# In-projection statistics from rows of x squared in their own layout, and the first loads and splits in another order

## The chip, the cores and the metric

The kernel runs on one core of a Trainium2 chip. A core has five engines with their own instruction streams: TensorE (PE in the profile, its weight loads PEld), VectorE (DVE), ScalarE (ACT), GpSimd (POOL) and SyncE (SP), which here only issues transfers (DMAs). They meet through semaphores. Operands lie in SBUF (128 partitions); products come out in PSUM, eight banks of 128x512 fp32.

The metric is the device time of one execution in microseconds (us). Three runs of the kernel before took 2518.49, 2518.77 and 2519.21 us: a median of 2518.77.

## The reference

One layer of an encoder over 2048 tokens of width 1024, with a memory of 256 tokens:

```python
xn = rmsnorm(h, g_mix[l])
z = jnp.einsum('bsd,dc->bsc', xn, w_in[l])          # q, k, v, p_in, f_logit
...                                                  # forgetting attention and multi-scale pool
h = h + jnp.einsum('bsc,cd->bsd', jnp.concatenate([fox, pool], axis=-1), w_out[l])
mn = rmsnorm(mem, g_mem_kv[l])
mkv = jnp.einsum('bmd,dc->bmc', mn, w_mem_kv[l])     # keys and values of the memory
...                                                  # cross-attention on the memory
...                                                  # SwiGLU
```

where `rmsnorm(x, g)` is x / sqrt(mean(x^2) + 1e-6) * g over the 1024 channels of a token. So each of the 2048 tokens of x, and each of the 256 of the memory, needs one number, the inverse root of the mean of its squares. The change is about how these numbers come about.

## The kernel before

All large products are computed in three passes: each operand is split into a high part (rounded to the fp32r format) and a low part (the rest), and `mm3` (lines 66 to 71) issues high by high, high by low and low by high. L69, L70 and L71 in the profile are these three passes, whatever the product. ACT makes the high part, DVE the low part (`split`, `split_gain`, L185 and L186, `sub_hi`, L64). The gains of the norms are multiplied into the weights while they are split; the token's own factor is multiplied on when a product leaves PSUM (`scaled`, L354), so a product may run before its statistics are known.

The stage in question has two parts. In the first, PE computes the memory's keys and values: tiles `kv00`, `kv01`, `kv10`, `kv11` (first digit: half of the 256 memory tokens; second: keys or values), each in its own bank, over eight steps k of 128 channels. Per step there are 12 matmuls of 128x512. The weights `w_mem_kv` come in eight loads of 512 KB (`load_kv`), and `split_kv` puts their parts in turn into `qs`, `kh` and `kl`. The memory comes transposed in four tiles of 256 KB (`x_load` with `memT`), each holding two steps. 22 warm-up matmuls on zeros stand ahead of it on PE.

The second part is the in-projection of x: 16 blocks of 128 tokens, each of 96 matmuls (four column groups `zps` of 384 or 392, eight steps k, three passes). x comes transposed, 256 tokens at a time, as four tiles (`x_load`), and `x_split` makes `xhi` and `xl` of them. So block i belongs to the pair b = i // 2. Its weights are eight loads of 772 KB (`load_w_in`), split by `split_w_in` into `wh` and `wl`. Block 0 (`zps0`) runs with k outermost, so that each step needs only the weights of that k; later blocks run column group by column group. The four `zps` tiles take over the four banks of the `kv` tiles: the first that of bank 4, the second bank 7, the third bank 6, the fourth bank 5; `kv00` to `kv11` lie in 4, 5, 6, 7 in the order in which line 225 makes them.

The statistics lie across the partitions of the transposed x, so they need a sum over partitions. `x_split` squares each tile on ACT (L167), POOL adds the four up into `part` (L169) and folds its two halves (L171), and `token_sums` multiplies `part` by a column of ones on PE (L211). `token_rstd` copies the two sums out of PSUM on DVE (L217) and takes the inverse root on POOL (L78, L80). For the memory the same stands at k=3, with its sums over `mpart`.

Between lines 223 and 576 all five engines follow the order in which the code is written (`in_order`); within that stretch each engine's stream is this order, and an instruction that waits holds all behind it on its engine. SP issues its loads and stores in this order too. After the stretch a scheduler sets the order on all engines but PE, whose order stays as written within the listed engines.

In the loop over blocks, per block: loads for later; the first column group of block i; the last transposes of block i-2; on even blocks `token_sums`; the other column groups; ACT's `scaled`; transposes of block i-1 (`to_heads`, L406); then `normed_heads`, and for even blocks `x_split` of the next pair, for odd ones a split of the pool weights `w_p`.

Of the kernel before, what the change touches and what calls it, by code (L numbers as in the profile page):

```python
# [16 lines left out]
P = 128  # L17
# [24 lines left out]
def block_kernel(ctx: ExitStack, tc: tile.TileContext, x, xT, memT, cols, rows, w_qkvf, w_p, w_pool, w_out,  # L42
# [116 lines left out]
    def x_split(tiles, part=None, qs=range(4), join=True):  # L159

        for q in qs:
# [3 lines left out]
            if part is not None:  # L165
                sq = xp.tile([P, 2, B], F32, tag="xsq", name="xsq", bufs=2)[:] if q else part
                act.activation(sq, raw[:], AF.Square, scale=1.0 / 32.0)  # L167
                if q:
                    pool.tensor_tensor(out=part, in0=part, in1=sq, op=ALU.add)  # L169
                if q == 3 and join:  # L170
                    pool.tensor_tensor(out=part[:, 0], in0=part[:, 0], in1=part[:, 1], op=ALU.add)  # L171
# [29 lines left out]
    with ExitStack() as c0:  # L201
# [4 lines left out]
        def token_sums(part, halves=1):  # L206

            ssp = tpp.tile([P, 2], F32, tag="ss", name="ss", bufs=1)
            for j in range(2):
                for c in range(halves):  # L210
                    pe.matmul(ssp[:, j:j + 1], lhsT=part[:, c, j * P:(j + 1) * P], rhs=ones[:, 0:1], start=c == 0,  # L211
                              stop=c == halves - 1)
            return ssp

        def token_rstd(ssp, outp):
            ms = xp.tile([P, 2], F32, tag="ms", name="ms", bufs=2)
            dve.tensor_copy(ms[:], ssp[:])  # L217
            rsqrt(outp, ms[:])


# [4 lines left out]
        kv = [[kvp.tile([P, MW], F32, name=f"kv{m}{a}") for a in range(2)] for m in range(2)]  # L225
# [8 lines left out]
        def load_kv(k):  # L234
            wk[k] = w_in_hi(k, F32)[:, :2 * MW]
            sp.dma_start(wk[k], w_mem_kv[k * P:(k + 1) * P, :])

        def split_kv(k):
# [3 lines left out]
            w_ = MW if k == 0 else 2 * MW  # L242
# [24 lines left out]
        for k in range(4):  # L267
            mt += x_load(0, memT.rearrange("(k p) m -> p k m", p=P), (k,))
            load_kv(k)
        xt = x_load(0)  # L270
        mpart = xp.tile([P, 2, B], F32, tag="part", name="part", bufs=1)
        mr = cst.tile([P, 2], F32, name="mr")
        for k in range(KD):
            if k == 0:
                raw = mt[0][1]
                x_split(mt, None, (0,))
# [13 lines left out]
            if k < 4:  # L290
                load_kv(k + 4)
            if k == 1:
                sp.dma_start(rowt[:], rows.partition_broadcast(P))
                load_w_in(0)
            if k == 3:
                for c in range(1, KD):
                    load_w_in(c)
# [42 lines left out]
        with ExitStack() as c1:  # L340
# [84 lines left out]
            def load_w_p(k):  # L425
# [3 lines left out]
                else:  # L429
                    raw = xp.tile([P, 2, B], F32, tag="xsq" if k == NPRE else "part", name="wpr",  # L430
                                  bufs=2 if k == NPRE else 1)
# [6 lines left out]
            def stat_diag(b):  # L438

                diag = xp.tile([P, 2, B], F32, tag="xsq", name="diag", bufs=2)[:, 0].rearrange("p (j t) -> p j t", j=2)  # L440
# [10 lines left out]
            def stat_rows(rbp):  # L451
                rb = xp.tile([P, 2, B], F32, tag="xsq", name="rbs", bufs=2)[:, 0]
# [49 lines left out]
            NPRE = 6  # L502
# [1136 lines left out]
```

## Time and profile before

| | |
|---|---|
| Median of three runs | 2518.77 us |
| Profiled execution | 2518.27 us |
| Its span, first to last instruction | 2516.6 us |
| Mean granted TensorE clock | 0.999 |
| PE busy | 2496.4 us |
| DVE, ACT, POOL busy | 1674.5, 1235.0, 800.5 us |
| First `kv` matmul starts | 6.56 us |
| First `zps` matmul starts | 34.46 us |
| Block 1's first matmul starts | 52.23 us |

Rows of the timeline give the start, the duration, the engine, the line and operation, the tile written, the tiles read, the shape and a count; in brackets stands how long the engine had been idle and what ended that. Where a count is over one, the duration spans all of them. Rows of groups give the total busy time in us and the mean of one instruction in ns, then the idle time ahead of them. Consecutive matmuls overlap: the step from one start to the next is their cost, not the duration.

### The profile page before, as it was taken

To read this page: it belongs to the slowest core of one execution; us is meant where nothing else is said; L and a number is where in the kernel's file an instruction comes from. 1 tells how busy PE (TensorE), PEld (TensorE's weight loads), DVE (VectorE), ACT (ScalarE), POOL (GpSimd) and SP (SyncE) were. 2 spreads that over 40 slices of the span, in tenths; PEclk is the share of its full clock that TensorE was granted. 3 is DMA by queue.
4 is the path that set the end of the run, shared out by engine and by line. 5 is a ranking of instruction groups with operands and counts; after the bars stand their busy time and mean duration, and the time that the engine had idled before them with its cause. 6 is when DMAs were issued, how large, how long until landed. Compare 5 with 4: busy or idle time off the path is not lost.

```text
span 2516.6 us, 36820 instructions
## 1 busy us (share of the span) xinstructions
PE 2496.4 (99%) x13055; PEld 2139.7 (85%) x13055; DVE 1674.5 (67%) x2971; ACT 1235.0 (49%) x2355; POOL 800.5 (32%) x1096
## 2 busy tenths in 40 slices
PE   9999999999999999999999999999999999999999
PEld 8999999878888878888888888888888888888887
DVE  7444485579999965545877787657776666665554
ACT  6454451069999945444634433335443333333443
POOL 3344310035655623334244454330001222212000
PEclk9999999999999999999999999999999999999999
DMA  6454475366665432223644554457673323325765
GB/s 249 155 155 130 122 239 168 130 189 159 149 184 155 111 115 80 75 88 126 236 178 168 184 181 167 163 206 265 225 256 106 109 99 125 112 97 183 239 205 205
DMA packets 209688, 408.25 MB, mean 162 GB/s; under 512 B 24928, under 2 KB 100448, under 8 KB 198624
## 3 DMA queue, kind: packets, MB, share of 16 engines
q1 hardware_dynamic: 179392, 309.41, 38.8%
q0 software_dynamic: 30112, 96.49, 10.6%
q8 instruction: 102, 1.67, 0.3%
q14 instruction: 82, 0.67, 0.1%
HBM read 277.24 MB, written 132.78 MB: 163 GB/s over the span
## 4 chain that ended last, share of the span: by engine, by line
PE 72%; issue 9%; DVE 2%; POOL 1%; ACT 1%; DMA 1%; POOLq 0%; SPq 0%; ACTq 0%; DVEq 0%
PE bk L71 14%; PE bk L69 14%; PE bk L70 14%; PE acc L865 5%; PE sps L791 5%; PE tp L56 4%; PE mmps L69 3%; PE mmps L71 3%; PE mmps L70 3%; PE oo L69 1%; PE oo L70 1%; PE oo L71 1%; PE zp L69 1%; PE zp L70 1%; PE zp L71 1%
## 5 line engine op out<-in xcount | busy, mean ns | idle before, releaser
L64 DVE TENSOR_TENSOR ww<-draw,ww 128x512 fp32r<-128x512 f32 x308 | 205.2, 705 | 156.1 <-ACT ww L190 155.8
L190 ACT CAST ww<-draw 128x512 fp32r<-128x512 f32 x308 | 179.5, 620 | 219.0 <-PE bk L71 168.0
L64 DVE TENSOR_TENSOR ww<-graw,ww 128x512 fp32r<-128x512 f32 x220 | 176.7, 809 | 108.5 <-ACT ww L190 108.2
L70 PE MATMUL bk<-ww,ww 128*128 128x512 f32 x616 | 239.8, 389 | 0.4 <-DVE ww L64 0.4
L71 PE MATMUL bk<-ww,ww 128*128 128x512 f32 x616 | 239.7, 389 | 0.0
L69 PE MATMUL bk<-ww,ww 128*128 128x512 f32 x616 | 239.6, 389 | 0.0
L190 ACT CAST ww<-graw 128x512 fp32r<-128x512 f32 x220 | 136.0, 622 | 178.1 <-PE bk L71 160.9
L64 DVE TENSOR_TENSOR pl<-tp,ph 128x512 fp32r<-128x512 f32 (+3 forms) x298 | 177.5, 599 | 25.8 <-ACT ph L902 25.0
L69 PE MATMUL zps<-wh,xhi 128*128 128x384 f32 (+1 forms) x512 | 174.4, 341 | 0.6 <-DVE qs L186 0.6
L70 PE MATMUL zps<-wl,xhi 128*128 128x384 f32 (+1 forms) x512 | 171.9, 336 | 0.0
L71 PE MATMUL zps<-wh,xl 128*128 128x384 f32 (+1 forms) x512 | 171.9, 336 | 0.0
L902 ACT CAST ph<-tp 128x512 fp32r<-128x512 f32 (+3 forms) x298 | 148.1, 519 | 10.2 <-PE tp L56 8.8
L1532 POOL DMA_DIRECT2D out_dram<-o x32 | 17.3, 540 | 382.1 <-DVE o L1529 380.1
L69 PE MATMUL bk<-qs,ww 128*128 128x512 f32 x352 | 137.9, 392 | 0.3 <-ACT s L1451 0.3
L71 PE MATMUL bk<-qs,ww 128*128 128x512 f32 x352 | 137.2, 390 | 0.9 <-DVE ww L64 0.9
L70 PE MATMUL bk<-kh,ww 128*128 128x512 f32 x352 | 136.9, 389 | 0.0
L70 PEld LDWEIGHTS bk<-ww,ww 128*128 128x128 f32 x616 | 115.6, 188 | 25.1 <-DVE ww L64 0.8
L69 PE MATMUL bk<-kl,ww 128*128 128x512 f32 x352 | 136.9, 389 | 0.0
L70 PE MATMUL bk<-cb,ww 128*128 128x512 f32 x352 | 136.9, 389 | 0.0
L71 PE MATMUL bk<-kl,ww 128*128 128x512 f32 x352 | 136.9, 389 | 0.0
L69 PEld LDWEIGHTS bk<-ww,ww 128*128 128x128 f32 x616 | 115.6, 188 | 23.9
L71 PEld LDWEIGHTS bk<-ww,ww 128*128 128x128 f32 x616 | 115.6, 188 | 23.9
(637 smaller groups left out, 7234.2 us busy)
## 6 DMA issues: line engine op xcount, KB each, us to landing
graw<-in_w_gu_dram SPq DMA_DIRECT2D x44, 1024.0 KB, 5.5
draw<-in_w_down_dram SPq DMA_DIRECT2D x66, 256.0 KB, 4.5
xl<-in_xT_dram SPq DMA_DIRECT2D x64, 256.0 KB, 4.9
qkT<-st SPq DMA_DIRECT2D x64, 256.0 KB, 2.7
wdr<-in_w_down_dram SPq DMA_DIRECT2D x22, 512.0 KB, 4.6
vd<-cb SPq DMA_DIRECT2D x16, 512.0 KB, 3.4
qs<-qkT SPq DMA_DIRECT2D x8, 1024.0 KB, 7.0
kh<-qkT SPq DMA_DIRECT2D x16, 512.0 KB, 8.6
```

The source lines that it names most:

```text
L56: return pe.transpose(out.bitcast(F32R), src, identr[:])
L64: (eng or dve).tensor_tensor(out=lo, in0=src, in1=f(hi), op=ALU.subtract)
L69: pe.matmul(ps, lhsT=sh, rhs=mh, start=first, stop=False, skip_group_check=goes_on)
L70: pe.matmul(ps, lhsT=sh, rhs=ml, start=False, stop=False, skip_group_check=goes_on)
L71: pe.matmul(ps, lhsT=sl, rhs=mh, start=False, stop=last, skip_group_check=goes_on)
L190: act.copy(hi, raw)
L791: pe.matmul(ps[:, :wn], lhsT=qs[:, i * P:(i + 1) * P], rhs=kk[:, 512 * c:512 * c + wn], start=(a == 0), stop=(a == 1))
L865: pe.matmul(acc[:, qa * P:], lhsT=v[:, j, :], rhs=pm[:, qa * P:], start=state["n"] == 1, stop=state["n"] == 2 * nk)
L902: act.copy(ph[:, sl], tp[:, sl])
L1532: pool.dma_start(out[rows_, cs], o)
```

## The change

- The squares for x are taken in x's own layout, tokens on partitions. `row_load` brings 128 rows of x (128x1024, 512 KB) into a single buffer `xrow`; `row_stat` squares them on ACT in place and has ACT sum along the row (`accum_out`), so the token's number is there without PE; POOL takes the inverse root. `row_load(i + 1)` stands at the head of block i, ahead of its other loads, and has to wait until the row before has been squared; `row_stat(i + 1)` stands behind `normed_heads` of block i.
- `x_split` only splits. POOL's additions, `token_sums` of x on PE and its copy on DVE are gone.
- For the memory the squares stay transposed, but are added up on DVE (`mem_square`), and its sums stand at k=6 (`mem_sums`, `mem_rstd`).
- The first loads: the memory's tiles are loaded one by one ahead of the weights of their steps, all `kv` weights come ahead of x, x ahead of the in-projection weights, and the first row stands behind the sixth of these. The weights of k=0 are loaded in two halves, those of k=0 and k=1 split in two halves.
- The first splits: memory tiles behind the weights at k=1, 3, 5; the four tiles of the first x one at a time, at k=6, at k=7 and after the in-projection weights of k=2 and 4; `more_constants` after all of them.
- The `kv` tiles are made in the order 00, 11, 10, 01. Their products keep their order.
- Two of the pool weights are loaded into the freed `xrow` in place of two other buffers, and two small tiles (`diag`, `rbs`) get smaller ones.

On PE, at the head of an even block of the loop (`tp` are the transposes of block i-2, `ss` the token sums, `zps` the products), before:

```order
L70 MATMUL zps<-wl_499,xhi 128x384
L71 MATMUL zps<-wh_498,xl_673 128x384
L406 MATMUL tp<-identr,kl 128x128 x4
L211 MATMUL ss<-ones,part 128x1 x2
L69 MATMUL zps<-wh_430,xhi 128x384
L70 MATMUL zps<-wl_431,xhi 128x384
L71 MATMUL zps<-wh_430,xl_651 128x384
```

and now:

```order
L70 MATMUL zps<-wl_490,xhi 128x384
L71 MATMUL zps<-wh_489,xl_657 128x384
L429 MATMUL tp<-identr,kl 128x128 x4
L69 MATMUL zps<-wh_426,xhi 128x384
L70 MATMUL zps<-wl_427,xhi 128x384
L71 MATMUL zps<-wh_426,xl_645 128x384
```

The two sums (four records in the profile) are gone from between the transposes and the products; each of these places lost them.

On DVE, from the weights of k=5 to the second in-projection weight (`qs`, `kh`, `kl` are low parts of the `kv` weights or, out of `kv`, of the memory's values, `xl` those of x or the memory, `wl` those of the in-projection weights), before:

```order
L186 SCALAR_TENSOR_TENSOR kl<-wh_281,colt,kl 128x1024
L64 TENSOR_TENSOR xl_391<-xl_225,xhi 128x512
L64 TENSOR_TENSOR xl_398<-xl_227,xhi 128x512
L64 TENSOR_TENSOR xl_405<-xl_229,xhi 128x512
L64 TENSOR_TENSOR xl_413<-xl_231,xhi 128x512
L186 SCALAR_TENSOR_TENSOR qs<-wh_308,colt,qs 128x1024
L186 SCALAR_TENSOR_TENSOR wl_431<-wl_284,colt,wh_430 128x1544
L186 SCALAR_TENSOR_TENSOR kh<-wh_341,colt,kh 128x1024
```

and now:

```order
L179 SCALAR_TENSOR_TENSOR kl<-wh_226,colt,kl 128x1024
L64 TENSOR_TENSOR xl_366<-xl_228,xhi 128x512
L217 TENSOR_TENSOR msq<-msq 128x512
L179 SCALAR_TENSOR_TENSOR qs<-wh_230,colt,qs 128x1024
L64 TENSOR_TENSOR xl_405<-xl_234,xhi 128x512
L179 SCALAR_TENSOR_TENSOR kh<-wh_232,colt,kh 128x1024
L230 COPY mms<-ss 128x2
L179 SCALAR_TENSOR_TENSOR wl_427<-wl_243,colt,wh_426 128x1544
L64 TENSOR_TENSOR xl_432<-xl_236,xhi 128x512
L179 SCALAR_TENSOR_TENSOR wl_435<-wl_245,colt,wh_434 128x1544
```

The four x splits no longer stand together ahead of the k=6 weights; the first in-projection weight is split after the last `kv` weight.

On SP, the end of the first loads (`wl` and `cb` are the in-projection weights, `xl` x transposed, `mkvd` the memory's values on their way out, `xrow` a row load), before:

```order
L251 DMA wl_351<-in_w_qkvf_dram 128x1544
L251 DMA wl_353<-in_w_qkvf_dram 128x1544
L251 DMA cb<-in_w_qkvf_dram 128x1544
L306 DMA gffn<-in_g_ffn_row_dram 128x8x1
L316 DMA mkvd<-qs 128x1024 x2
L155 DMA xl_623<-in_xT_dram 128x2x256
```

and now:

```order
L268 DMA wl_253<-in_w_qkvf_dram 128x1544
L204 DMA xrow<-in_x_dram 128x1024
L268 DMA wl_257<-in_w_qkvf_dram 128x1544
L268 DMA cb<-in_w_qkvf_dram 128x1544
L326 DMA gffn<-in_g_ffn_row_dram 128x8x1
L336 DMA mkvd<-qs 128x1024 x2
L204 DMA xrow<-in_x_dram 128x1024
L155 DMA xl_615<-in_xT_dram 128x2x256
```

A row stands ahead of the last two in-projection weights, and the next row, which waits for ACT, ahead of the second pair's x.

The diff, cut to its core:

```diff
-    def x_split(tiles, part=None, qs=range(4), join=True):
+    def x_split(tiles, qs=range(4)):
...
             act.copy(hi[:], raw[:])
-            if part is not None:
-                sq = xp.tile([P, 2, B], F32, tag="xsq", name="xsq", bufs=2)[:] if q else part
-                act.activation(sq, raw[:], AF.Square, scale=1.0 / 32.0)
-                if q:
-                    pool.tensor_tensor(out=part, in0=part, in1=sq, op=ALU.add)
-                if q == 3 and join:
-                    pool.tensor_tensor(out=part[:, 0], in0=part[:, 0], in1=part[:, 1], op=ALU.add)
...
+        def row_load(i):
+
+            xrows[i] = xp.tile([P, D], F32, tag="xrow", name="xrow", bufs=1)
+            sp.dma_start(xrows[i][:], x[i * P:(i + 1) * P, :])
+
+        def row_stat(i):
+            ms = xp.tile([P, 1], F32, tag="ms", name="ms", bufs=2)
+            row = xrows.pop(i)[:]
+            act.activation(row, row, AF.Square, scale=1.0 / 32.0, accum_out=ms[:])
+            rsqrt(rstd[:, i:i + 1], ms[:])
+
+        def mem_square(q, raw):
+            sq = zp.tile([P, 4, P], F32, tag="st", name="msq", bufs=4)[:].rearrange("p a c -> p (a c)")
+            act.activation(sq, raw.rearrange("p a c -> p (a c)"), AF.Square, scale=1.0 / 32.0)
+            msq.append(sq)
+            if q:
+                dve.tensor_tensor(out=msq[0], in0=msq[0], in1=sq, op=ALU.add)
...
-        kv = [[kvp.tile([P, MW], F32, name=f"kv{m}{a}") for a in range(2)] for m in range(2)]
+        kv_ = {ma: kvp.tile([P, MW], F32, name=f"kv{ma[0]}{ma[1]}") for ma in ((0, 0), (1, 1), (1, 0), (0, 1))}
+        kv = [[kv_[m, a] for a in range(2)] for m in range(2)]
...
-            sp.dma_start(wk[k], w_mem_kv[k * P:(k + 1) * P, :])
+            w_ = MW if k == 0 else 2 * MW
+            for c in range(0, 2 * MW, w_):
+                sp.dma_start(wk[k][:, c:c + w_], w_mem_kv[k * P:(k + 1) * P, c:c + w_])
...
-            w_ = MW if k == 0 else 2 * MW
+            w_ = MW if k < 2 else 2 * MW
...
-        for k in range(4):
-            mt += x_load(0, memT.rearrange("(k p) m -> p k m", p=P), (k,))
+        load_mt = lambda q: mt.extend(x_load(0, memT.rearrange("(k p) m -> p k m", p=P), (q,)))
+        for k in range(KD):
+            if k == 0:
+                load_mt(0)
             load_kv(k)
+            if k % 2 and k < KD - 1:
+                load_mt((k + 1) // 2)
         xt = x_load(0)
-        mpart = xp.tile([P, 2, B], F32, tag="part", name="part", bufs=1)
+        sp.dma_start(rowt[:], rows.partition_broadcast(P))
+        for k in range(KD):
+            load_w_in(k)
+            if k == 5:
+                row_load(0)
...
-            elif k < 4:
-                x_split(mt, mpart[:], (k,), False)
             wh, wl = split_kv(k)
             if k == 0:
-                act.activation(mpart[:], raw[:], AF.Square, scale=1.0 / 32.0)
+                mem_square(0, raw[:])
+            elif k % 2 and k < KD - 1:
+                q = (k + 1) // 2
+                raw = mt[q][1]
+                x_split(mt, (q,))
+                mem_square(q, raw[:])
             mh, ml = x_part(mt, k)
-            if k == 3:
-                token_rstd(token_sums(mpart, 2), mr[:])
+            if k == 6:
+                ssp = mem_sums()
+            elif k == 7:
+                mem_rstd(ssp, mr[:])
...
             if k == 6:
+                x_split(xt, (0,))
+            if k == 7:
                 split_w_in(0)
-            if k == 7:
-                more_constants()
-            if k == 5:
-                part = xp.tile([P, 2, B], F32, tag="part", name="part", bufs=1)
-                x_split(xt, part[:])
+                x_split(xt, (1,))
...
-            ssp = token_sums(part)
             for k in range(2, KD):
                 split_w_in(k)
-            token_rstd(ssp, rstd[:, 0:2])
+                if k in (2, 4):
+                    x_split(xt, (k // 2 + 1,))
+                if k == 5:
+                    row_stat(0)
+            more_constants()
...
+                    if i + 1 < NT:
+                        row_load(i + 1)
                     if j == 0:
                         xt = x_load((b + 1) % NB)
...
-                        if j == 0:
-                            ssp = token_sums(part)
...
-                        if j == 0:
-                            token_rstd(ssp, rstd[:, i:i + 2])
...
+                    if i + 1 < NT:
+                        row_stat(i + 1)
                     if j == 0:
-                        if b + 1 < NB:
-                            part = xp.tile([P, 2, B], F32, tag="part", name="part", bufs=1)
-                            x_split(xt, part[:])
-                        else:
-                            x_split(xt)
+                        x_split(xt)
```

More of the change, by code (lines that the diff above doesn't have):

```diff
@@ L429, in load_w_p @@
                 else:
-                    raw = xp.tile([P, 2, B], F32, tag="xsq" if k == NPRE else "part", name="wpr",
-                                  bufs=2 if k == NPRE else 1)
+                    if k == NPRE:
+                        wprs.append(xp.tile([P, KD - NPRE, 4, P], F32, tag="xrow", name="wpr", bufs=1))
+                    raw = wprs[0][:, k - NPRE]
                 w_raw[k] = raw[:].rearrange("p a c -> p (a c)")
@@ L573, in block_kernel @@
             pT = columns(0, zs, rb, None)
[L574 removed]
+            x_split(xt, range(2, 4))
             zr = head_parts(*st_)
```

32 lines of the change are left out of this document (13 added, 19 removed).

## The prediction

> **What bounds the kernel now.** I read the page's busy shares first, then who TensorE (PE) waited for, then the timeline of the first 60 us, which is the only place where the change moves work.
>
> ```profile
> span 2516.6 us, 36820 instructions
> PE 2496.4 (99%) x13055; PEld 2139.7 (85%) x13055; DVE 1674.5 (67%) x2971; ACT 1235.0 (49%) x2355; POOL 800.5 (32%) x1096
> PE kv L70 <- DVE qs L186: 1.8, 2, 1.5
> PE kv L70 <- DVE kh L186: 1.2, 2, 0.8
> PE tp L406 <- ACT st L408: 0.7, 2, 0.5
> PE zps L69 <- DVE qs L186: 0.6, 1, 0.6
> 40.00:60.00 20.00, 20.00 (x119) 19.96 (x118) 14.77 (x17) 12.20 (x18) 7.29 (x8) 1.00 0.23 74
> ```
>
> PE is busy for 99% of the span, so only two things save time: fewer PE instructions, or less of the 20 us in which PE stands. The waits (line waited for, total us, times, longest) are from the first 480 us: 3.6 us of them lie in the memory keys and values (`kv`) and the first projection (`zps`). The last row is a window; its first busy column is PE: 20.00 of 20.00 us. From 40 us on the in-projection has no PE gap to give back, and what other engines save there is worth nothing by itself.
>
> **The sums by products in the loop.** Around each even block:
>
> ```profile
> 75.10 0.45 PE L406 MATMUL tp<-identr,kl 128*128 128x128 f32 x4
> 75.39 0.57 PE L211 MATMUL ss<-ones,part 128*128 128x1 f32 x4
> 75.83 0.43 PE L69 MATMUL zps<-wh,xhi 128*128 128x384 f32 x1
> 93.75 0.45 PE L406 MATMUL tp<-identr,kl 128*128 128x128 f32 x4
> 94.04 0.41 PE L69 MATMUL zps<-wh,xhi 128*128 128x384 f32 x1
> ```
>
> With the sums, the step from the transposes to the next projection is 75.83 - 75.10 = 0.73 us; in an odd block, without them, 94.04 - 93.75 = 0.29. One group of four records costs 0.44 us. Seven stand in the loop (blocks 2, 4 to 14): 7 x 0.44 = **3.1 us**, all on PE's path. That is the firm term. The eighth, ahead of `zps0`, is in the head below. The memory's own eight records stay and only move from k=3 to k=6.
>
> **What the loop gets in their place.** Per block one row load (512 KB on SP), one square over 128x1024 with its accumulator read on ScalarE (ACT), two small POOL operations for one column of `rstd`. Gone per pair of blocks are four ACT squares, four POOL additions and a DVE copy.
>
> ```profile
> L1239 ACT ACTIVATE hn<-h 128x1024 f32<-128x1024 f32 x12 | 12.6, 1052 | 0.3 <-DVE h L1230 0.3
> L1157 ACT ACTIVATION_READ_ACCUMULATOR hT<-h 128x1 f32 x16 | 3.0, 187 | 0.0
> L167 ACT ACTIVATE xsq<-xl 128x512 f32<-128x512 f32 x21 | 13.5, 645 | 21.5 <-POOL part L169 21.5
> ```
>
> ACT: 2 x (1.05 + 0.19) = 2.5 us new per pair, against 4 x 0.645 = 2.6 old: even. The 21.5 us that ACT stood for POOL's additions goes too, but PE never waited on it there (the window above), so I cost the loop's other parts at nothing. Their cover is the 33.6 us that PE needs for a pair of blocks.
>
> **The head.** It runs from the first `kv` matmul to the second block's first matmul.
>
> ```profile
> 2.04 4.29 PE L265 MATMUL warm<-cb 128*128 128x256 f32 x22 [2.04 <-POOL cb L262]
> 6.56 0.50 PE L69 MATMUL kv<-qs,xhi 128*128 128x512 f32 x1 [0.23 <-ACT qs L185]
> 20.55 0.40 PE L69 MATMUL kv<-kh,xhi 128*128 128x512 f32 x1
> 23.35 0.40 PE L69 MATMUL kv<-kl,xhi 128*128 128x512 f32 x1
> 42.26 0.33 PE L69 MATMUL zps<-wh,xhi 128*128 128x384 f32 x1
> 44.36 0.33 PE L69 MATMUL zps<-wh,xhi 128*128 128x384 f32 x1
> 52.23 0.34 PE L69 MATMUL zps<-wh,xhi 128*128 128x384 f32 x1
> ```
>
> Twelve `kv` matmuls take 23.35 - 20.55 = 2.80 us, twelve of `zps` 44.36 - 42.26 = 2.10. The head holds 96 of each: 22.4 + 16.8 = 39.2 us. It lasts 52.23 - 6.56 = 45.7, so 6.5 us are not products. Where they are:
>
> ```profile
> 21.77 5.10 POOL L169 TENSOR_TENSOR part<-part,xsq 128x512 f32<-128x512 f32 x3 [2.64 <-ACT xsq L167]
> 20.85 4.88 DVE L64 TENSOR_TENSOR xl<-xl,xhi 128x512 fp32r<-128x512 f32 x4
> 25.66 2.30 DVE L186 SCALAR_TENSOR_TENSOR qs<-wh,colt,qs 128x1024 fp32r<-128x1024 f32 x1
> 28.02 0.50 PE L70 MATMUL kv<-qs,xhi 128*128 128x512 f32 x1 [1.47 <-DVE qs L186]
> 9.94 1.28 DVE L186 SCALAR_TENSOR_TENSOR kh<-wh,colt,kh 128x1024 fp32r<-128x1024 f32 x1 [1.07 <-ACT kh L185]
> 35.02 0.75 DVE L186 SCALAR_TENSOR_TENSOR qs<-kv,mr,qs 128x512 fp32r<-128x512 f32 x1 [0.58 <-ACT qs L185]
> 35.83 0.44 PE L69 MATMUL zps<-wh,xhi 128*128 128x384 f32 x1 [0.60 <-DVE qs L186]
> ```
>
> All four splits of the first x block stand in one lump ahead of the k=6 weights, and beside POOL's additions DVE is slow: 4.88 / 4 = 1.22 us per subtraction, and the k=6 split takes 2.30 where the same form took 1.28 at 9.94. PE waits 1.47 us for it. At the end the second `zps` tile takes over the PSUM bank of `kv11`, the last to be emptied (35.02 + 0.75 = 35.77), and starts at 35.83.
>
> After the change POOL has no additions; the x splits stand one by one among the weights; the two halves of `wk1` are split apart; the second `zps` tile sits on `kv01`'s bank, emptied second. Step by step, as an estimate from these rows:
>
> Start: the 22 warm-up matmuls end at 2.04 + 4.29 = 6.33. Halving the first weight load can't bring PE further forward than that: 6.35, a gain of 0.2 however early the half lands.
>
> Steady `kv`: for two k, PE needs 5.6 us; DVE 2 x 1.28 for weights plus one subtraction and one addition, priced like the 0.69 us of a lone subtraction (row below): 3.9. DVE keeps ahead, and so I expect the 1.47 us wait and its follower at k=7 to go. At k=2 DVE has two half weights, a subtraction and an addition ahead of it; I take 0.35 us of waiting there, between 0 and 0.8.
>
> The memory's eight sum records cost twice 0.44, 0.9 us. So `kv` ends at 6.35 + 22.4 + 0.9 + 0.35 = 30.0.
>
> In `zps0` DVE's split of the weights becomes the close one.
>
> ```profile
> 36.49 9.50 DVE L186 SCALAR_TENSOR_TENSOR wl<-wl,colt,wh 128x1544 fp32r<-128x1544 f32 x5 [0.72 <-ACT wh L185]
> 34.89 7.47 ACT L185 ACTIVATE wh<-wl,colt 128x1544 fp32r<-128x1544 f32 x5
> 58.30 0.69 DVE L64 TENSOR_TENSOR xl<-xl,xhi 128x512 fp32r<-128x512 f32 x1 [0.24 <-ACT xhi L164]
> 22.11 0.33 SPq L251 DMA_DIRECT2D cb<-in_w_qkvf_dram  x1
> cb<-in_w_qkvf_dram SPq DMA_DIRECT2D x1, 772.0 KB, 14.6
> 25.00:30.00 5.00, 3.53 (x16) 2.55 (x15) 5.00 (x3) 4.17 (x4) 3.40 (x3) 1.00 1.01 420
> ```
>
> ACT drains the last `kv` bank until 30.7 and makes `wh2` by 32.2 (7.47 / 5 = 1.5). DVE then needs 6 x 1.9 + 2 x 0.69 = 12.8 us and ends at 45.0; PE comes to k=7 at 30.0 + 7 x 2.1 = 44.7. They run neck and neck: I take 0.5 us of waits, between 0 and 0.9. ACT, with the row's square (1.24 us) between k=5 and k=6, ends near 42, ahead of both.
>
> `zps0` then ends at 30.0 + 16.8 + 0.5 = 47.3, against 52.23: **4.9 us**.
>
> Loads: the last weight lands at 22.1 + 14.6 = 36.7 now. The row adds 0.52 MB ahead of it, 1.25 us at the 420 GB/s of the window (last column): 38.0. ACT asks for it near 40.5. So the new load is covered by some 2.5 us; with that cover gone PE would wait for it. The reordered loads put every `kv` weight earlier than now.
>
> The Trainium skill, "DMA: Bandwidth & Descriptors", section "Anatomy of one DMA — SWDGE (gpsimd) path", speaks against more and smaller loads: it gives each a fixed cost of about 2.0 us beside its bytes, there for transfers that GpSimd issues. If the two extra loads ahead of the last weight (half a weight, a row) paid that in full, it would land at 42.0 as an estimate by that page, 1.5 us after it is asked for, and the sum would be 6.5 instead of 8.0. The window's 420 GB/s with 772 KB transfers shows such costs overlapped, so the sum above leaves it out.
>
> Past 340 us the order differs in few places (one `rb` product stands ahead of the last four transposes, a `pT` later on DVE); PE waited 0.7 us at transposes there (first fence). I take 0, between a gain of 0.5 and a loss of 0.5.
>
> **Sum.** 3.1 + 4.9 = 8.0 us. The profiled execution took 2518.27 (span 2516.6 and 1.67 around it), so 2510.3; the median of the runs stands 0.5 higher, hence **2510.8**.
>
> **Rivals.**
>
> First: chains stay tight in `zps0`. The last weight comes late, or the memory's keys do: DVE normalises them after its last weight split.
>
> ```profile
> 46.08 1.83 DVE L186 SCALAR_TENSOR_TENSOR wl<-cb,colt,wh 128x1544 fp32r<-128x1544 f32 x1
> 53.20 0.69 DVE L326 TENSOR_TENSOR mks<-mks,mkr 128x512 f32<-128x512 f32 x1 [1.40 <-POOL mkr L80]
> 56.40 1.04 PE L333 MATMUL tp<-ident,mks 128*128 128x128 f32 x8
> ```
>
> The keys have 56.4 - 53.9 = 2.5 us of slack today; with PE 4.9 us earlier and DVE's last split only 2.9 earlier (46.08 + 1.83 = 47.9, to 45.0), about 0.5 is left. Both late by 1 us: 2.0 lost, 2512.8. The Trainium skill's fixed cost would bring the first half of this about.
>
> Second: the head gives nothing: some wait of the same size takes the place of those removed, and only the loop's 3.1 us stay: 2518.77 - 3.1 = 2515.7. For it: three engines run close there. Against it: the waits are put down to DVE work that moves or shrinks.
>
> Third, slower: SP is one queue, and each row load waits on it until ACT has squared the row before; the x loads of the next pair stand behind it.
>
> ```profile
> 73.80 2.56 SPq L155 DMA_DIRECT2D xl<-in_xT_dram  x4
> 92.11 0.64 ACT L164 CAST xhi<-xl 128x512 fp32r<-128x512 f32 x1
> ```
>
> Today x is issued at 73.8 to 76.4 and first cast at 92.1, 15.7 us after the last issue. The square ends perhaps 1.5 us later than the issue today. Only if SP were held more than some 10 us would x be late; 2 us lost at each of seven pairs would give 14, so 2518.8 - 8.0 + 14 = 2524.8.
>
> That the change doesn't do what it says is excluded on PE: the `ss` records are gone from its order.
>
> **How the numbers follow.** My forecast 0.75, rival 1 0.11, rival 2 0.09, the slower rival 0.05. The range: 2509.4 if the waits taken as 0.35 and 0.5 are zero and the transposes gain 0.5 (8.0 + 0.85 + 0.5 = 9.35); 2513.4 if they are 0.8 and 0.9, the transposes lose 0.5, keys and loads lose 1.0 together and a sum group saves 0.4 (8.0 - 0.85 - 0.5 - 1.0 - 0.3 = 5.35). That takes in the forecast and rival 1. Faster by over 0.2% (5.0 us, about what a measurement here can tell from no change) means below 2513.7: 0.86. Within 0.2%: rival 2, 0.09. Slower: 0.05.
>
> **What would show it.** No `ss` records in the loop and 0.29 us from transposes to products in even blocks; first `kv` matmul near 6.35; no wait over 0.5 us at k=6; first `zps` product near 30.0 with the second tile close behind it; second block's first product near 47.3; gap-free PE from there to 310 us. Wrong would be a PE wait for `wh`/`wl` of k=5 to 7, for the transposed `mks`, or for `rstd`'s scaling inside the loop.

## The result: 3.3 us faster, less than half of what was forecast

After the change the kernel takes 2514.73 us (median; 2513.98 to 2517.04), beside 2518.07 before (2516.98 to 2520.15), measured together on one chip. The ratio is 0.9987, with a 95% interval of 0.9981 to 0.9993: faster, by 0.13%, which is within the 0.2% that the prediction called no change. It had 2510.8 us, with a range of 2509.4 to 2513.4.

The profiled execution took 2514.7 us with a span of 2513.0, so 3.6 us less than the one before. Page, list of TensorE's waits up to 480 us, and the window from 40 to 60 us, after the change:

```profile
span 2513.0 us, 36744 instructions
PE 2495.9 (99%) x13023; PEld 2140.8 (85%) x13023; DVE 1657.7 (66%) x2967; ACT 1235.6 (49%) x2356; POOL 773.4 (31%) x1077
PE warm L282 <- POOL cb L279: 2.0, 1, 2.0
PE tp L429 <- ACT st L431: 1.1, 1, 1.1
40.00:60.00 20.00, 20.00 (x119) 19.89 (x119) 16.14 (x21) 11.43 (x18) 11.07 (x9) 1.00 0.60 201
```

PE has 32 records fewer. All waits for `qs` and `kh` in the head are gone here; the first 340 us hold none but the one ahead of the warm-up. A second profile of this kernel has one of 0.3 us for `qs` among the first products. The window stays without a gap. One even block of the loop, and the head, in the timeline of PE:

```profile
70.59 0.46 PE L429 MATMUL tp<-identr,kl 128*128 128x128 f32 x4
70.88 0.41 PE L69 MATMUL zps<-wh,xhi 128*128 128x384 f32 x1
...
2.04 5.07 PE L282 MATMUL warm<-cb 128*128 128x256 f32 x22 [2.04 <-POOL cb L279]
6.90 0.63 PE L69 MATMUL kv<-qs,xhi 128*128 128x512 f32 x1
30.61 0.34 PE L69 MATMUL zps<-wh,xhi 128*128 128x384 f32 x1
31.17 0.44 PE L69 MATMUL zps<-wh,xhi 128*128 128x384 f32 x1
47.71 0.34 PE L69 MATMUL zps<-wh,xhi 128*128 128x384 f32 x1
```

From the transposes to the products it is 0.29 us now, where it was 0.73. The second block's first product stands at 47.71 instead of 52.23: the head gave 4.5 us.

So the gain was there, and was lost again. To see where, I matched PE's instructions one by one between traces. The offset is the start of an instruction in a profile of the kernel before, minus its start in the other trace. The table has two profiles of the kernel after (the second comes from the third experiment) against the second profile of the kernel before (from the fourth); the first profile of before stands beside them to show how far two profiles of one kernel differ.

| at (us of before) | before, first profile | after, first | after, second |
|---|---|---|---|
| 47, end of the head | -0.2 | 4.4 | 3.9 |
| 297, end of the loop | -0.2 | 7.6 | 7.1 |
| 500, pooling projection done | -0.2 | 6.1 | 6.1 |
| 630 | -0.2 | 6.1 | 6.0 |
| 640 | -0.2 | 4.7 | 4.5 |
| 780 | -0.2 | 4.5 | 4.0 |
| 1100 | -0.5 | 4.5 | 3.9 |
| 1300 | 0.0 | 3.5 | 4.1 |
| end | 0.0 | 3.5 | 3.5 |

Of 7.1 to 7.6 us, 1.1 to 1.5 go slowly between 297 and 500 us, 1.4 to 1.6 at once between 630 and 640 (0.2 of it comes back by 700), 0.4 to 0.7 near 770, and the rest further on. In none of these places does PE have other instructions than before; near 340 us a few stand in another order.

**The slow loss.** It lies in the pooling projection (`zp`, matmuls of 128x256). The first and the last of one group of 96 in the timeline of PE, before and after:

```profile
476.25 0.28 PE L69 MATMUL zp<-xhi,wph 128*128 128x256 f32 x1
487.38 0.28 PE L71 MATMUL zp<-xhi,wpl 128*128 128x256 f32 x1
```

```profile
469.77 0.28 PE L69 MATMUL zp<-xhi,wph 128*128 128x256 f32 x1
481.17 0.28 PE L71 MATMUL zp<-xhi,wpl 128*128 128x256 f32 x1
```

11.13 us for 95 steps is 117.2 ns; 11.40 is 120.0. The same 96 matmuls, gap-free in both, are 2.4% slower. What differs is where their operands stand in SBUF: the new tile `mms` makes the pool `xp` 32 bytes larger. That puts the low parts `xl` (all buffers but the last) and all that follows in the pools on that side 32 bytes away from where it was. The buffers of `xhi` moved by 2016 bytes, 32 less than the size of one buffer, because the tiles beside them changed as well.

**The loss at once.** The waits of PE from 600 to 660 us hold one row after the change, and none before. Then POOL's timeline ahead of it, after the change:

```profile
PE acc L886 <- POOL pl L64: 0.8, 1, 0.8
```

```profile
624.64 1.57 POOL L866 TENSOR_TENSOR fo<-fo,lbs 128x512 f32<-128x512 f32 x1 [2.34 <-ACT fo L856]
627.86 0.86 POOL L871 DMA_DIRECT2D catT<-fo  x1 [1.65 <-DMA catT<-fo]
630.81 1.27 POOL L64 TENSOR_TENSOR pl<-pf,ph 128x512 fp32r<-128x512 f32 x1
```

and the same place before:

```profile
630.86 1.56 POOL L845 TENSOR_TENSOR fo<-fo,lbs 128x512 f32<-128x512 f32 x1 [2.33 <-ACT fo L835]
632.36 0.87 POOL L850 DMA_DIRECT2D catT<-fo  x1
```

POOL adds half of `fo` onto `catT` by DMA, and must wait until SP's store of the other half has landed. That store (issued at 621.6 after, 627.8 before, right behind a load of 1 MB of `v` and one of 256 KB of `lbs`) lands in 5.7 us after the change and in 3.9 before. POOL stands 1.65 us, everything behind it on its queue is late, `pl` with it. PE waits 0.83 us, and with the short gaps around this wait it is 1.4 us late. The DMA traffic of the 4 us around the end of the burst (629.7 to 633.7 before, 623.5 to 627.5 after), in 40 slices of 0.1 us, before the change:

```profile
GB/s 492 144 410 594 184 266 369 430 410 389 389 287 307 185 287 103 0 0 0 0 0 0 0 0 0 0 0 0 0 0 0 0 0 0 0 0 0 0 143 184
```

and after it:

```profile
GB/s 82 410 594 266 184 328 471 328 410 369 348 246 369 205 205 0 0 0 0 0 0 0 20 0 20 0 20 0 20 21 20 20 20 0 0 0 0 0 143 184
q8 instruction: 1, 0.02, 1.5%
q14 instruction: 1, 0.01, 0.7%
```

After the change the burst ends in the fifteenth slice, and after a pause one packet at a time comes through for 1.1 us: one of the 16 DMA engines is late. In the trace a packet of 16384 bytes on queue 8 starts at 624.76 and takes 0.95 us; the late packets follow it. I take queue 8 to bring PE's program: the page has 102 such packets, 1.67 MB, for 13023 matmuls and as many weight loads, which makes 64 bytes each and one packet for some 127 matmul records.

```profile
q8 instruction: 102, 1.67, 0.3%
```

The Trainium skill, "DMA: Bandwidth & Descriptors", section "Queues, rings and completion order", says that a DMA engine takes work from its queues in turn, a whole packet at a time; and the section "Why a DMA increments its semaphore by 16 and not by 1" says that a DMA counts as complete only when every engine that it runs on is. The row of GB/s agrees with both: one engine with a 16 KB packet ahead of its last 2 KB ones holds up the whole store.

With 32 records fewer ahead of it, a packet boundary of PE's program falls 32 records later in the work. Before the change the packet near this place was fetched at 622.45, 3.1 us ahead of the burst's first issue; after it at 624.76, 5.5 us behind that issue. At some 19 us a packet here, 32 of 127 records make some 5 of these 8.5 us; the rest was not explained.

### The profile page after: what moved, and what is told of

It is laid out like the page before. It is cut to its first block, busy times and chain, and to the rows that moved or that the text cites. A ratio compares the mean times of both kernels' runs of the same rounds, so it can differ in the third digit from the quotient of the medians.

```text
span 2513.0 us, 36744 instructions
## 1 busy us (share of the span) xinstructions
PE 2495.9 (99%) x13023; PEld 2140.8 (85%) x13023; DVE 1657.7 (66%) x2967; ACT 1235.6 (49%) x2356; POOL 773.4 (31%) x1077
## 3 DMA queue, kind: packets, MB, share of 16 engines
q8 instruction: 102, 1.67, 0.3%
## 4 chain that ended last, share of the span: by engine, by line
PE 74%; issue 9%; DVE 2%; DMA 1%; POOL 1%; ACT 1%; SPq 0%; POOLq 0%; DVEq 0%; ACTq 0%
PE bk L69 14%; PE bk L71 14%; PE bk L70 14%; PE acc L886 5%; PE sps L812 5%; PE tp L56 4%; PE mmps L69 3%; PE mmps L71 3%; PE mmps L70 3%; PE oo L70 1%; PE oo L71 1%; PE oo L69 1%; PE zp L71 1%; PE zp L70 1%; PE zp L69 1%
## 5 line engine op out<-in xcount | busy, mean ns | idle before, releaser
L69 PEld LDWEIGHTS bk<-ww,ww 128*128 128x128 f32 x616 | 115.7, 188 | 24.2
L1553 POOL DMA_DIRECT2D out_dram<-o x32 | 17.3, 540 | 382.1 <-DVE o L1550 380.1
```

What stands on the lines that cost most here:

```text
L69: pe.matmul(ps, lhsT=sh, rhs=mh, start=first, stop=False, skip_group_check=goes_on)
L1553: pool.dma_start(out[rows_, cs], o)
```

## The experiments

Five theories were set against each other. A: the place of x in SBUF sets the pace of `zp`. F: the packets of PE's program, shifted by the missing records, collide with the loads. Against them B: the later waits take back what is gained ahead of them, whatever its source; W: the waits at 632 and 770 us come from the work standing earlier against other loads; and C: chance differences between executions. A profile is one execution; the medians are of 10 or 11 runs (one run where it is said), and the kernel before stood beside them at 2518.43 to 2518.49 us.

**After, with x moved 32 bytes on.** The expectation takes this to be its place before. It isn't: the edit moves x on in the direction in which the change had moved it, to 64 bytes from there.

```diff
-            ms = xp.tile([P, 2], F32, tag="mms", name="mms", bufs=1)
+            ms = xp.tile([P, 2], F32, tag="mms", name="mms", bufs=2)
```

> The kernel after with 32 bytes more in the pool of x (the mean square of the memory has two buffers instead of one), so that the parts of x, the pool weights and all that stands in the pools on that side lie 32 bytes further on, as they lay in the kernel before; no instruction differs. Theory A (where the parts of x lie sets how fast TensorE reads them in the pooling projection): the steps of its 128x256 products between 340 and 490 us go from 0.120 back to between 0.116 and 0.119 us, and with some 630 of them in that stretch the whole is about 1.5 us faster than the kernel after, near 2513.2. Theory B (the given-back time is only in waits and in the clock past 600 us): the steps stay at 0.120, and the time stays within 0.5 us of 2514.7. Theory C (the shares differ from one execution to the next): the steps differ between two profiles of the same kernel as much as between these.

2515.42 us (2514.14 to 2517.55), ratio 0.9989 (0.9980 to 0.9998): no faster than the kernel after. The steps did change: 118.4 ns in the group of 96, with a mean of 120.0 from 400 to 500 us instead of 121.3, and 0.9 us lost from 349 to 500 us instead of 1.2 to 1.4. Theory A holds in part on the steps and fails on the time, since near 770 us this run lost 1.1 us instead of 0.4 to 0.7.

**Before, with x moved 32 bytes.**

```diff
-            ms = xp.tile([P, 2], F32, tag="ms", name="ms", bufs=2)
+            ms = xp.tile([P, 2], F32, tag="ms", name="ms", bufs=3)
```

> The kernel before with 32 bytes more in the pool of x (the mean square has three buffers instead of two), so that the parts of x lie as in the kernel after; no instruction differs. Theory A (the place of the parts of x sets the pace of the pooling projection): its 128x256 products step at 0.120 us instead of 0.116 to 0.119, the whole is some 1.5 us slower than the kernel before, near 2519.6, and the rest is as it was. Theories B and C: within 0.5 us of the kernel before, and steps as there.

2519.78 us (2518.44 to 2521.52), ratio 1.0005 (0.9996 to 1.0014). The time points to A without being clear of no change; the steps are clear:

```profile
478.37 0.28 PE L69 MATMUL zp<-xhi,wph 128*128 128x256 f32 x1
489.76 0.28 PE L71 MATMUL zp<-xhi,wpl 128*128 128x256 f32 x1
```

11.39 us, 119.9 ns, in a kernel without any of the change; from 341 to 500 us it lost 1.6 us against the kernel before.

**After and before again, unchanged**, for second profiles.

> The kernel after, unchanged, for a second profile of it. If what it gives back later is a matter of its order (theory B), the wait of 1.78 us for ScalarE's s near 1249 us and the stretch at half the clock behind it stand here again, with the wait near 632 us. If it is a matter of single executions (theory C), the second profile has other stalls at other places, and its offsets against the profile of before past 600 us differ by more than 1 us from the first one's. The first 300 us are the same in both, with 7.5 to 7.9 us gained by 297 us. 2514.7, between 2514.0 and 2517.0.

> The kernel before, unchanged, for a second profile of it. Theory B: no wait over 1 us for ScalarE's s near 1250 us and no stretch at half the clock there. Theory C: stalls at other places than in the first profile, moving by 1 us or more. 2518.1, between 2517.0 and 2520.2.

2515.08 us (2514.28 to 2516.88; ratio 0.9987, 0.9978 to 0.9996) and 2518.22 (one run). Theory C falls for the two losses: the pace of `zp` and the wait at 632 us stand in both profiles of after and in neither of before, and their ends agree with the first ones' within 0.1 us. It holds for the stretch near 1250 us, where B had expected the same stall again. The windows of the first and of the second profile of after (columns: PE, PE's weight loads, DVE, ACT, POOL, granted clock, DMA share, GB/s):

```profile
1250.00:1254.00 4.00, 4.00 (x13) 3.10 (x11) 4.00 (x5) 3.31 (x6) 3.61 (x4) 0.57 0.95 403
```

```profile
1250.00:1254.00 4.00, 4.00 (x19) 3.28 (x18) 3.08 (x6) 3.97 (x7) 3.19 (x2) 1.00 1.00 424
```

A wait for ScalarE's `s` stands there in every profile, 0.3 and 1.6 us before, 1.8 and 1.2 after; in one of these four the clock fell to about half behind it. The first profile of after lost 0.9 us there against the second of before, the second lost none, so I put none of the loss down to the change.

**After, with 32 records put back as a longer warm-up.**

```diff
-        for n in range(22):
-            pe.matmul(wps[:], lhsT=warm[:, :P], rhs=warm[:, :B], start=True, stop=True)
+        for n in range(54):
+            pe.matmul(wps[:, :48], lhsT=warm[:, :P], rhs=warm[:, :48], start=True, stop=True)
```

> The kernel after with 54 warm-up matmuls of 48 columns in place of 22 of 256, so that TensorE's program has 32 matmul records more ahead of everything else, as many as the change took out. Theory F (TensorE's program is fetched by DMA in packets of 16384 bytes, one for some 127 matmul records; with 32 records fewer each packet falls 32 records later in the work, and the one at 624.8 us now falls into the burst of v, lbs and catT): the packet falls ahead of that burst again, the catT store issued at 621.6 lands in 3.9 to 4.2 us instead of 5.7 to 5.9, GpSimd's wait of 1.65 to 1.83 us for it and TensorE's wait of 0.83 us for pl are gone, and the loss of 1.4 us at 631 to 640 us and of some 0.5 at 770 to 780 is made good: 1.4 to 2.0 us faster than the kernel after, near 2513.3, if the shorter warm-up costs the head nothing. Theory W (those waits come from the work standing earlier against other loads): they stay, and the time stays at 2514.9 within 0.5.

2521.00 us (2519.11 to 2524.31), ratio 1.0010 (1.0001 to 1.0019): a miss on the time, through a mistake in the experiment.

```profile
2.04 11.71 PE L282 MATMUL warm<-cb 128*128 128x48 f32 x54 [2.04 <-POOL cb L279]
```

A warm-up matmul of 48 columns takes 0.217 us in the mean of the stretch, hardly less than the 0.230 of one of 256 (5.07 / 22), so the head began 6.7 us late. PE also stayed slow longer: the first thirteen `kv` products step at 0.43 us or more, where later ones step at 0.23, and at 36 us the run is 8.9 us behind the kernel after. What the run was made for it shows all the same: the catT store lands in 3.8 us, the wait for `pl` is gone, and from 500 to 846 us the offset stays at -2.5, where the kernel after lost 1.5 and 2.1.

**After, with x where it was before.**

```diff
-            ms = xp.tile([P, 2], F32, tag="mms", name="mms", bufs=1)
+            ms = xp.tile([P, 2], F32, tag="ms", name="mms", bufs=2)
```

> The kernel after with the memory's mean square in one of the two buffers of the tokens' mean square instead of a buffer of its own: the pool of x is 32 bytes smaller, and the low parts of x, the last pool weights and what follows stand at the very addresses of the kernel before. Theory A (the place of the parts of x sets the pace of the pooling projection): the 128x256 products step at 0.119 us in the mean of 400 to 500 us as before, not at 0.1213, and the stretch from 349 to 500 us gives 1.0 to 1.3 us back, with 2513.8 for the whole. If instead the distance between high and low parts counts (the high parts stand 2048 bytes from their place before), the mean is 0.120 as in the run with 32 bytes more, and the gain is 0.5 us.

2515.09 us (2513.51 to 2517.49), ratio 0.9985 (0.9977 to 0.9994): as fast as the kernel after. But the pace of `zp` is that of before to the nanosecond:

```profile
469.86 0.28 PE L69 MATMUL zp<-xhi,wph 128*128 128x256 f32 x1
480.99 0.28 PE L71 MATMUL zp<-xhi,wpl 128*128 128x256 f32 x1
```

11.13 us, 117.2 ns, a mean of 118.9 from 400 to 500 us as in the kernel before, and 0.2 us lost from 349 to 500. What was won went near 770 us: 1.4 us, where after lost 0.4 and 0.7. There the packet of PE's program fell 4.9 us behind the issue of `v`, and the store took 5.8 us, where in the two profiles of after it fell 3.3 and 3.4 us behind it, and the store took 4.8 and 5.1. So the second loss hid what mending the first one gave, here and in the first experiment.

**Both edits together.**

> Both edits on the kernel after: 54 short warm-up matmuls and the memory's mean square in a buffer of the tokens'. Theories A and F together: the two gains add, 1.0 to 1.3 and 1.4 to 2.0, so 2.4 to 3.3 us faster than the kernel after, near 2512.0, and the distance to the kernel before at 980 us is within 1 us of that at 297 us. Theory B (late waits absorb what is gained earlier, whatever its source): the gains at 500 and 640 us are there, but the wait for ScalarE's s near 1250 us grows by as much, and the end stays near 2514.5.

2519.98 us (2518.27 to 2524.95), ratio 1.0005 (0.9996 to 1.0014). The late head is in it again, so it decides nothing on the sum. The pace of `zp` is 117.2 ns, and from 500 to 846 us the offset goes from -6.98 to -7.10. Its profiled execution, the slow end of its runs, lost 6.5 us more at 380 us, waiting for a load of x; I didn't pursue that.

**After, with idle products where the sums were.**

```diff
                             mem_keys()
+                        if j == 0:
+                            idle = tpp.tile([P, 2], F32, tag="ss", name="ss", bufs=1)
+                            for n in range(2):
+                                pe.matmul(idle[:, n:n + 1], lhsT=ones[:], rhs=ones[:, 0:1], start=True, stop=True)
                         zps.update(project(i, j, hs, ls, range(1, 4)))
```

> The kernel after with two idle products of 128x1 put where the kernel before had its sums in the second block of each pair (four records, seven places), their results unused: TensorE does the work again that the change took from the loop. By the prediction's sum alone the whole is 3.1 us slower than the kernel after, 2518.0. Theory F: the offset at 297 us falls by 3.1, but with 28 of 32 records put back the packets of TensorE's program fall nearly where they did before, the waits at 632 and 770 us go, and the whole is only 1.1 to 1.7 us slower, near 2516.3. Theory W: the waits stay, 2518.0.

2516.92 us (2515.47 to 2520.16), ratio 0.9994 (0.9985 to 1.0002). From 47 to 297 us the offset grows by 0.0, where the kernel after's grew by 3.2: the loop's term is what the prediction made it. The whole is only 1.8 us slower, near F's 1.1 to 1.7 and far from 3.1: from 500 to 846 us it loses 0.2.

**After, with 33 records put back at no cost**: eleven of the memory's products are cut into halves of 256 columns.

```diff
-                    as_ = slice(a * MW, (a + 1) * MW)
-                    mm3(kv[m][a][:], (mh[:, ms_], ml[:, ms_]), (wh[:, as_], wl[:, as_]), k == 0, k == KD - 1)
+                    halves = 2 if k in (4, 5) or (k == 6 and (m, a) != (1, 1)) else 1
+                    w_ = MW // halves
+                    for c in range(halves):
+                        as_ = slice(a * MW + c * w_, a * MW + (c + 1) * w_)
+                        mm3(kv[m][a][:, c * w_:(c + 1) * w_], (mh[:, ms_], ml[:, ms_]), (wh[:, as_], wl[:, as_]),
+                            k == 0, k == KD - 1)
```

> The kernel after with 11 of the memory's products (three matmuls each, at k of 4 to 6) cut into two halves of 256 columns: the same columns, and 33 matmul records more in TensorE's program ahead of the loop, without the longer warm-up that spoiled the run with 54 warm-ups. Theory F: the packets of TensorE's program fall where they do in the kernel before, the catT stores behind v at 619 and 757 us land in 3.5 to 4.3 us, the waits for pl at 632 and 770 are gone, and the offset to the kernel before falls by no more than 0.2 us from 500 to 846 us, where the kernel after lost 1.5 to 2.1. At most 0.3 us is lost in the head. The whole: 1.2 to 1.8 us faster than the kernel after, near 2513.4. Theory B (later waits absorb what is gained earlier): the offset is kept up to 1200 us, but the end stays at 2514.9 within 0.5.

2513.70 us (2511.78 to 2515.44), ratio 0.9980 (0.9971 to 0.9988): 1.4 us less than the kernel after had in its second set of runs. The offset goes from 5.40 at 500 us to 5.23 at 846. The place where the kernel after lost 1.4 us, in POOL's timeline, and the DMA traffic of the 4 us that answer to those shown above:

```profile
625.39 1.57 POOL L870 TENSOR_TENSOR fo<-fo,lbs 128x512 f32<-128x512 f32 x1 [2.32 <-ACT fo L860]
626.89 0.85 POOL L875 DMA_DIRECT2D catT<-fo  x1
```

```profile
GB/s 389 123 492 348 184 287 266 328 348 369 369 389 226 225 123 41 0 0 0 0 0 0 0 0 0 0 0 0 0 0 0 0 0 0 0 0 0 0 20 205
q14 instruction: 1, 0.01, 0.7%
```

POOL doesn't wait, no packet of queue 8 is in the window, and nothing trails the burst. The store lands in 3.8 us.

**Both, without the longer warm-up**: the halves of the ninth run and the place of x of the sixth.

> The same cut in the kernel after with the memory's mean square in a buffer of the tokens', so that the parts of x stand as in the kernel before too. Theories A and F together: an offset to the kernel before of 6.2 to 7.5 us from 297 to 980 us, losing less than 0.5 between, and 2511.5 to 2512.5 for the whole, which is faster than both kernels and what the prediction's sum came to within 1.5 us. Theory B: the offset is there at 980 us, but what stands between 1217 and 1262 us takes over 1.5 us of it, and the whole is over 2513.5.

2512.28 us (2511.64 to 2517.10), ratio 0.9977 (0.9969 to 0.9986): the fastest of all, 2.8 us below the kernel after. Its offset is 6.25 at 297 us, 6.32 at 500, 6.14 at 846, 6.03 at 1100 and 6.23 at the end. What is gained in the first 300 us arrives at the end; theory B is out. This run and the sixth also decide against W: they differ in the halves alone and are equally far ahead of the kernel before at 630 us (6.3 us), but the sixth loses 1.3 us by 640 us and this one nothing. So it isn't that the work stands earlier.

**The reverse: before, with all the memory's products from k=1 on in halves**, 84 records more.

```diff
-                    as_ = slice(a * MW, (a + 1) * MW)
-                    mm3(kv[m][a][:], (mh[:, ms_], ml[:, ms_]), (wh[:, as_], wl[:, as_]), k == 0, k == KD - 1)
+                    halves = 2 if k else 1
+                    w_ = MW // halves
+                    for c in range(halves):
+                        as_ = slice(a * MW + c * w_, a * MW + (c + 1) * w_)
+                        mm3(kv[m][a][:, c * w_:(c + 1) * w_], (mh[:, ms_], ml[:, ms_]), (wh[:, as_], wl[:, as_]),
+                            k == 0, k == KD - 1 and c == halves - 1)
```

> The reverse: the kernel before with all the memory's products from k = 1 on cut into halves, 84 matmul records more. With one packet for some 127 records that is as if 43 had been taken out, and the packets fall some 43 records later in the work than before, into the bursts behind v at 625 and 762 us. Theory F: at one or both of them the catT store lands in 4.8 to 5.9 us instead of 3.7 to 4.2, GpSimd waits for it, a wait for pl of some 0.8 us appears on TensorE, and 0.4 to 2 us are lost from 630 to 780 us, in a kernel that has none of the change; with up to 0.7 us for the halves in the head, 2519.2 to 2520.9. Theory W (the waits come from the work standing earlier): no such wait, 2518.4 to 2519.1.

2519.27 us (2518.66 to 2522.41), ratio 1.0003 (0.9994 to 1.0012). The time lies within F's range, but not for F's reason: the offset is -0.5 at 47 us and still -0.7 at 846. (The profiled execution, the slowest of its eleven, lost 3.0 us more near 1250 us, at a wait of 3.6 us for `s`.) On what it was made for, F misses. The packet came where it should, 5.4 us behind the issue of `v` at 625.9, and is in the window that answers to the one above:

```profile
GB/s 102 492 471 246 410 328 369 389 410 369 389 389 225 246 123 82 41 0 0 0 0 0 0 0 0 0 0 0 0 0 0 0 0 0 0 0 0 0 143 184
q8 instruction: 1, 0.02, 1.4%
```

But nothing trails, the store landed in 4.0 us, and no wait for `pl` followed. So a packet within the burst isn't enough. In four profiles of kernels that hold the edited code (after, twice, and the first and sixth runs) the store behind the packet at 619 us was late each time, with 5.7 to 5.9 us; in this run, and at other heads' bursts with packets 5.2 to 5.7 us behind the issue, two of them in the kernel before (580 and 716 us), it was not. My guess is that the packet has to fall on an engine that still has parts of the store to move; the records don't name the engine of a packet, so what decides this stays open.

## Why the prediction was wrong

The steps that it worked out held:

- *Loop, 3.1 us.* Offsets grew by 3.2 from 47 to 297 us in both profiles, and 0.29 us stands between transposes and products. The row loads and squares cost nothing, as assumed: windows stay full and x was never late, so the slower rival didn't come up.
- *Start of the head, 6.35.* It was 6.90: the warm-up took 5.07 us in this execution instead of 4.29. Its steps stay at 0.21 us to the last, where in the profile before the last six take 0.12. The length isn't the change's doing: in the second run, the kernel before with one small buffer more, the first `kv` product starts at 6.91 too. Offsets at 36 us differ by up to 0.9 us between profiles of kernels with the same head.
- *Waits in `kv`.* The 1.47 us and its follower went, and the 0.35 expected at k=2 didn't come. `kv` took 30.61 - 6.90 = 23.7 us, against 22.4 + 0.9 + 0.35 = 23.65: the same sum for another reason, since the first matmuls ran slower (0.63 us busy for the first, against 0.40 later). In the second profile `kv` took 24.2 us, with 0.3 us of waiting and other short gaps among the first products; the prediction had no wait there.
- *`zps0`.* 47.71 - 30.61 = 17.1 us, against 17.3; the second tile follows 0.56 behind the first. Neither the last weight nor the memory's keys came late, so the first rival is out. The fixed cost that the Trainium skill gives each DMA ("DMA: Bandwidth & Descriptors", "Anatomy of one DMA — SWDGE (gpsimd) path") did not show either: by it PE would have stood 1.5 us for the last weight, and it did not stand. The head gave 4.5, against 4.9.

The step that failed is the last: "Past 340 us the order differs in few places … I take 0, between a gain of 0.5 and a loss of 0.5." From 297 us to the end it was -4.0 and -3.6 in the two profiles. That term looked at order and waits alone. What moved there were two things that order doesn't show: the places of tiles in SBUF, by 32 bytes (1.2 to 1.4 us, of which the sixth run got 1.1 to 1.3 back), and where PE's program is fetched in the work (1.5 to 2.1 us from 500 to 846 us, of which the ninth run got all but 0.2 back). Mended together they make 2512.28 us, within the range forecast and 1.5 above its value. Of that, the head of the tenth run has 0.9 to 1.3 us less offset at 47 us than the kernel after; the spread of the start covers most of it, and the halves up to 0.3.

The second rival, that only 3.1 us stay, came nearest in time (2515.7), but by luck: its mechanism did not happen, since the head gave nearly what it was to give.

The remaining 0.5 to 1.0 us, from 846 us to the end, aren't settled. The two profiles of the kernel after themselves differ there by half a microsecond.

## What to carry to other kernels

Before costing a change's untouched stages at zero, compare the addresses of the tiles that they read and count the instructions that were added or taken ahead of them; both are known before a run, though the count tells only that a fetch of the program moves, not whether it will hurt. A new tile, however small, is best put into a buffer that exists already, or where nothing stands behind it. When a gain vanishes downstream, match the traces instruction by instruction and look for the places where the offset falls; then mend each by an edit that costs nothing, and more than one at once, because one loss can hide what mending the other gives.

## What the hardware showed that was not expected

- A shift of 32 bytes in SBUF moved the pace of 128x256 matmuls between 117.2 and 119.9 ns, in both kernels and both ways, in gap-free stretches. The other matmuls whose pace I compared (`zps`, which have x as the stationary side, and `kv`) kept theirs, 173 and 232 ns. The weight loads of the slowed products lengthened too, from 188 to 192 ns in the median. The Trainium skill, "SBUF — State Buffer", section "A bandwidth-pool intuition that's wrong (but worth ruling out)", gives PE a second, independent read port for weight loads; by that alone the two paces would be equal, and the measurement decides. Which addresses collide was not worked out: 64 bytes from the old place it was 118.4. It isn't the distance between the two operands: the pool weights of k=6 and 7 moved by the same 32 bytes as `xl`, those of the other k stayed, and in the slow place all step at 120 ns.
- Fetching the program is DMA traffic beside the kernel's own: 16 KB for some 127 matmul records, about 1 us on one engine. A change of 32 records out of 13055 moved one such packet into a burst and cost 1.4 us there; other bursts took such a packet without loss.
- In the warm-up a 48-column matmul took no less than one of 256 columns: both step at 0.213 us. The means of 0.217 and 0.230 us over the whole stretch hold the longer first step and the last product as well.
